# Hybrid attention block on one core: side work behind a step's transposes, an earlier split of the plain values, modulation sums closed later, more products ahead of the last heads

## The chip, the cores and the metric

The kernel runs on one core of one Trainium2 chip. The metric is device time in microseconds (us) of one execution; the time before is the median of three runs. The engines are called PE (matrix products and transposes, with PEld for its weight loads), DVE (vector), ACT (scalar), POOL (GpSimd) and SP (which issues the transfers).

## The reference

One layer of a backbone block over 512 latent tokens and 256 context tokens, width 1024, all in float32. What matters of it:

```
sh1, sc1, g1, sh2, sc2, g2 = split(silu(c) @ w_mod + b_mod, 6)
h, hc = modulate(rms_norm(x), sh1, sc1), modulate(rms_norm(ctx), csh1, csc1)
qa, ka, va, hy, qd, kd, vd = split(h @ w_in)          # and the context's from hc
ya = softmax(qa [ka_c, ka]^T) [va_c, va]              # 4 plain heads, 2 shared key/value heads
yd = (softmax(q1 k1^T) - lam softmax(q2 k2^T)) vd     # 4 differential heads, 768 keys
yh = hyena(hy)                                        # long convolutions
y  = concat(rms(ya), rms(yh), rms(yd) * 0.8) @ w_out
x  = x + g1 * y
a, v = split(modulate(rms_norm(x), sh2, sc2) @ w_up)
out = x + g2 * ((gelu(dwconv3(a)) * v) @ w_down)
```

Each differential head has two softmax components. "d" in the kernel's names stands for the differential heads, "a" for the plain ones, "h" for Hyena.

## The kernel before, in words

**Products.** Most products are made in three parts: each operand is split into a "hi" part in fp32r (a cast, mostly on ACT, `hi_of`, L72) and a "lo" part, what is left of it (a subtraction on DVE or POOL, `lo_of`, L80); `mm3` (L82 to L85) adds hi·hi, lo·hi and hi·lo. So whatever comes from PE as an operand of a later product takes the way PE, ACT (hi), DVE (lo), PE.

**Stages.** Filters and transforms of Hyena; then Hyena and the input projection woven together (chunks q0 to q7, each for the latent rows, L, and the context, C), to about 280 us; then the attention steps, to about 392; then the output projection with what is left of the heads; then the feed-forward half, from 439 us to the end.

**Modulation's sums.** The projections of c for g1, sh2 and sc2 are matrix-vector products. `mod2_step` (L715) makes one of 24 pieces each time it is called: it loads 512 KB of w_mod (mraw, two buffers), and DVE adds it, scaled, into macc (L732, eight to a column group). When a group is full, its closing products stand due: eight small PE matmuls (mc, L737), which add over the partitions, and an addition into mcol on DVE (L738). `MOD_AT` says how many pieces come per chunk. Before the change the closing comes two calls after the last piece, and the call between does nothing (`pause`).

**Early heads.** Three attention steps of the first differential head run inside the projection's chunks 6 and 7, with tiles named se (scores), mxe (maximum) and pe (exponential). Their scores have one PSUM buffer, so the scores of the next component wait until ACT has made the exponential of the last.

**Attention steps.** The steps are a list: 16 for the d heads (four heads, four blocks of 128 queries, two components each), then those of the a heads. The loop over n (L1141 to L1173) works in a pipeline: step n's scores and exponentials, the combination of the two components of step n-1 on POOL, the transposes of step n-3, the products with the values of step n-5. In the form for n < 16 a step is, for each component jj: scores on PE (sd, L745/L746), the maximum over 768 keys on DVE (mxd, L749), the exponential on ACT (pd, L750); and for each half of step n-3: three transposes on PE (Td, L1055) into one PSUM tile and ACT's copy of it into SBUF (atd, L72). `values` (L1072) is six matmuls into yd. From n = 16 on (`late`) the order is another one; the change doesn't touch it.

**Side work.** Beside the steps run generators, started at given steps, which `advance()` moves on by one `yield` each; it is called twice a step. They are: `prepare` (from `PREP_AT`: transposes of the next head's q and k, qTd, kT0d, kT1d, hi casts qhld and khd, lo's, transfers into the stacked tiles), `y_out` (transposes yT, hi and lo of a finished output Y), `finish_d` (ysbd, ynd, ysqd, s4d: the norm of a d head), `split_va` (from `VA_AT`: hi and lo of the plain heads' values, va into vas), and `finish_a`. Typically a generator's PE and ACT part falls into a step's first call and its DVE part into the second.

**PSUM.** All transposes, those of the steps (Td) and those of the side work (qT, kT, yT, yn), take tiles of one tag with three buffers (`ps_t`). Scores have two, the heads' outputs one.

**What sets the order.** Within the attention loop and the tail the instructions of PE, DVE and ACT run in the order in which the code issues them (`manual_schedule`); before it, in that of a scheduler with the code's order as its guide. POOL's and SP's rows are ordered by the framework. Each engine works through its row in order.

**Tail.** After the loop, 24 partial products of the output projection (`fill`, `accumulate`, three matmuls o each) are dealt out by `TAIL` between calls of `advance()`, so many ahead of each. In between, the last a head is finished: DVE multiplies yna by the row's norm sa (L1006), PE transposes it (yTa, L940), ACT and DVE make Y. Weights of the output projection are loaded and split in units (`wo_unit`: or, oh, ol); `WO_LO` names for each of eight units the engine of its lo, p for POOL and v for DVE.

Of the kernel before, what the change touches and what calls it, by code (L numbers as in the profile page):

```python
# [8 lines left out]
F32 = mybir.dt.float32  # L9
F32R = mybir.dt.float32r  # L10
AF = mybir.ActivationFunctionType
ALU = mybir.AluOpType
# [2 lines left out]
NOSYNC = mybir.DependencyInfo(mybir.DependencyClass.NoSync, mybir.DependencyReason.DATA)  # L15

P = 128
WO_LO = "ppppvvvv"

D_C, D_T, D_V = 1, 3, 5  # L20
LATE = 16
EARLY = 3
MOD_AT = (0, 0, 0, 2, 2, 2, 2, 2, 2, 2, 2, 2, 2, 2, 0, 0)
PREP_AT = (4, 7, 12, 17)
VA_AT = 13
HY_AT = (5, 6)
WO_AT = (24, 26, 28)
TAIL = (2, 0, 0, 0, 0, 0, 7, 0, 0, 2)
UP_AT, UP_AHEAD, UP_NEXT, UP_LAG = 4, 5, 5, 2
D = 1024  # L30
T = 512
# [13 lines left out]
def block_kernel(tc, x, ctxt, small, ffs, wmod1, wmod2, whyd, wqkvd, woutd, wupd, wdownd,  # L45
# [668 lines left out]

    def mod2_step():  # L715

        if m2s.pop("pause", False):
            return
        if "due" in m2s:
            m2s.pop("due")()  # L720
        n = m2s["n"]
        if n == m2s["end"]:
            return
        m2s["n"] = n + 1
        g, k = n // NK, n % NK
        r = m2s["pl"].tile([P, D], F32, tag="mr", bufs=2, name=f"mraw{g}{k}")
        dma(r, wmod2[g, k])
        if k == 0:
            m2s["a"] = m2s["pl"].tile([P, D], F32, tag="ma", bufs=1, name=f"macc{g}")
            V.tensor_scalar(m2s["a"], r, sv[:, 0:1], None, ALU.mult)  # L730
        else:
            V.scalar_tensor_tensor(m2s["a"], r, sv[:, k:k + 1], m2s["a"], ALU.mult, ALU.add)  # L732
        if k == NK - 1:
            def due(a=m2s["a"]):
                t0 = m2s["ps"](f"mc{g}")
                for i in range(NK):
                    T_.matmul(t0[:, 2 * i:2 * i + 2], a[:, i * P:(i + 1) * P], ones[:, 0:2], start=True, stop=True)  # L737
                V.tensor_tensor(mcol[:, g], t0[:, 0:16:2], cols[:, C_BM + 8 * g:C_BM + 8 * g + 8], ALU.add)  # L738
            m2s["due"], m2s["pause"] = due, True

    def scores(s, qs, ks, kz, j, tt):

# [240 lines left out]
    def finish_a(b, yps):  # L983
        V.reciprocal(rra[:, :, 2 * b:2 * b + 2], sta[:, :, 2 * b:2 * b + 2])
        ysb = y3(f"ysba{b}")
        S.copy(ysb, yps)
        yield
        yn0 = natural(f"a{b}", ysb)
        yield
        yn = att.tile([P, 4, 2, 64], F32, name=f"yna{b}")  # L990
        V.tensor_tensor(yn, yn0.rearrange("p (a j d) -> p a j d", a=4, j=2),
                        rra[:, :, 2 * b:2 * b + 2].unsqueeze(3).broadcast_to([P, 4, 2, 64]), ALU.mult)
        yield
        sq = y3(f"ysqa{b}").rearrange("p (a c) -> p a c", a=4)
        S.activation(sq, yn.rearrange("p a j d -> p a (j d)"), AF.Square)
        yield
        V.tensor_reduce(sa[:, b], sq, AX.X, ALU.add)
        yna[b] = yn
        if b == 1:
            V.tensor_tensor(sa[:, 0], sa[:, 0], sa[:, 1], ALU.add)  # L1000
            rstd_of(sa[:, 2], sa[:, 0], 256, 4)
            yield
            yield
            for b_ in range(2):
                yv = yna[b_].rearrange("p a j d -> p a (j d)")
                V.tensor_tensor(yv, yv, sa[:, 2].unsqueeze(2).broadcast_to([P, 4, P]), ALU.mult)  # L1006
                yield
                yield from y_out(b_, f"a{b_}", lambda tt: yv[:, tt])

# [89 lines left out]
    def wo_unit(n_):  # L1099
        r = wp.tile([P, D], F32, tag="wr", bufs=3, name=f"or{n_}")  # L1100
        dma(r, woutd[n_])
        if n_ in (2, 7):
            h = wx.tile([P, 2, D], F32R, tag="x", bufs=1, name=f"ox{n_}")
            h, l = h[:, 0], h[:, 1]
        else:
            pl, tg = (dp, "o") if n_ in (3, 4) else (wp, "w")
            h = pl.tile([P, D], F32R, tag=tg + "h", bufs=2, name=f"oh{n_}")
            l = pl.tile([P, D], F32R, tag=tg + "l", bufs=2, name=f"ol{n_}")
        hi_of(h, r, "a")
        lo_of(l, r, h, WO_LO[n_])  # L1110
        wo[n_] = h.rearrange("p (k c) -> p k c", k=2), l.rearrange("p (k c) -> p k c", k=2)

    def po_of(tt, n):
# [20 lines left out]
    while n < len(steps) + D_V:  # L1134
# [10 lines left out]
        if late:  # L1145
            if on(D_T):
                for hh in range(2):
                    transposes(n - D_T, held[n - D_T][0], hh)
                held.pop(n - D_T)
            if n - 1 in waiting:  # L1150
                held[n - 1] = waiting.pop(n - 1)()
            if on(D_C):
                combine(n - D_C, held[n - D_C])
            while later:
                later.pop(0)()
            advance()
            if on(D_V):
                values(n - D_V)
            if on(0):
                waiting[n] = front(n, 0)  # L1160
        else:
            held[n] = front(n, 0)()
            if on(D_C):
                combine(n - D_C, held[n - D_C])
            advance()
            if on(D_T):
                transposes(n - D_T, held[n - D_T][0], 0)
            held[n] += front(n, 1)()
            if on(D_T):
                transposes(n - D_T, held.pop(n - D_T)[0], 1)  # L1170
            if on(D_V):
                values(n - D_V)
        advance()  # L1173
# [302 lines left out]
```

## Time and profile before

| | |
|---|---|
| median of three runs (lowest, highest) | 819.24 us (816.74, 821.53) |
| the profiled execution's own time | 818.88 us |
| its span in the trace | 817.1 us |
| mean granted clock of PE | 0.981 |
| PE busy in the span | 95% |
| DVE, ACT, POOL busy | 58%, 39%, 25% |
| attention steps 3 to 15 (279.71 to 342.00) | 62.29 us, PE busy 51.87 |
| late attention steps (342.00 to 391.60) | 49.60 us, PE busy 49.24 |
| from there to 439.00 (tail, output projection) | 47.40 us, PE busy 45.10 |

A row of the timeline gives the start in us, the duration in us, the engine, the line, the operation, and what it writes and reads; xN means N alike in a row, whose duration is that of all. In square brackets stands how long the engine had been idle, and what ended that. A row of the waits reads: who waited, for what, us in total, how many times, the longest. A row of a stretch gives its bounds, its length, the busy us of each engine with the number of instructions, PE's granted clock (1.00 is full speed), the share of the transfers and GB/s; a row with one number ahead of the clock is for PE alone. Durations of rows that follow each other on one engine overlap by about 0.1 us, so costs are read from start to start. PE's ends are modelled.

### The profile page before, as it was taken

To read this page: it belongs to the slowest core of one execution; us is meant where nothing else is said; L and a number is where in the kernel's file an instruction comes from. 1 tells how busy PE (TensorE), PEld (TensorE's weight loads), DVE (VectorE), ACT (ScalarE), POOL (GpSimd) and SP (SyncE) were. 2 spreads that over 40 slices of the span, in tenths; PEclk is the share of its full clock that TensorE was granted. 3 is DMA by queue.
4 is the path that set the end of the run, shared out by engine and by line. 5 is a ranking of instruction groups with operands and counts; after the bars stand their busy time and mean duration, and the time that the engine had idled before them with its cause. 6 is when DMAs were issued, how large, how long until landed. Compare 5 with 4: busy or idle time off the path is not lost.

```text
span 817.1 us, 11113 instructions
## 1 busy us (share of the span) xinstructions
PE 776.7 (95%) x4334; PEld 655.9 (80%) x4334; DVE 476.5 (58%) x679; ACT 318.5 (39%) x546; POOL 201.7 (25%) x190
## 2 busy tenths in 40 slices
PE   5888999999998988899899999999999999999997
PEld 1246889999997877799788988888888888888886
DVE  5555578886876777778376594444444333333325
ACT  1464434323122477778254343332333232332320
POOL 0652506757950556622151000000000000000000
PEclk8698999999999999999999999999999999999999
DMA  8901232114675332412352183232223323232202
GB/s 326 384 3 59 96 129 79 53 31 152 219 231 188 85 90 66 116 26 79 129 187 75 52 270 104 91 103 103 91 89 103 103 77 104 78 104 99 82 26 103
DMA packets 30701, 93.68 MB, mean 115 GB/s; under 512 B 5639, under 2 KB 8022, under 8 KB 29625
## 3 DMA queue, kind: packets, MB, share of 16 engines
q1 hardware_dynamic: 30649, 92.98, 34.4%
q8 instruction: 34, 0.56, 0.3%
q14 instruction: 18, 0.15, 0.1%
HBM read 83.79 MB, written 2.10 MB: 105 GB/s over the span
## 4 chain that ended last, share of the span: by engine, by line
PE 81%; DVE 8%; ACT 4%; POOL 2%; DMA 2%; issue 2%; SPq 0%; ACTq 0%; DVEq 0%; POOLq 0%
PE u L84 5%; PE u L83 5%; PE u L85 5%; PE dn L85 5%; PE dn L84 5%; PE dn L83 5%; PE uv L83 2%; PE ua L85 2%; PE uv L84 2%; PE uv L85 2%; PE ua L83 2%; PE ua L84 2%; PE yd L1072 2%; DMA mraw<-in_dram 2%; PE f L384 2%
## 5 line engine op out<-in xcount | busy, mean ns | idle before, releaser
L80 DVE TENSOR_TENSOR ul<-ur,uh 128x1024 fp32r<-128x1024 f32 x62 | 75.9, 1224 | 101.9 <-ACT uh L72 101.0
L72 ACT CAST uh<-ur 128x1024 fp32r<-128x1024 f32 x66 | 69.2, 1051 | 116.3 <-PE u L84 90.6
L83 PE MATMUL u<-h2h,uh 128*128 128x512 f32 (+1 forms) x224 | 81.2, 363 | 0.0
L85 PE MATMUL u<-h2h,ul 128*128 128x512 f32 (+1 forms) x224 | 80.3, 359 | 0.0
L84 PE MATMUL u<-h2l,uh 128*128 128x512 f32 (+1 forms) x224 | 80.3, 359 | 0.0
L84 PE MATMUL dn<-ul,gh 128*128 128x512 f32 x176 | 69.6, 396 | 0.0
L85 PE MATMUL dn<-uh,gl 128*128 128x512 f32 x176 | 69.6, 396 | 0.0
L83 PE MATMUL dn<-uh,gh 128*128 128x512 f32 x176 | 69.3, 396 | 0.0
L80 DVE TENSOR_TENSOR gl<-gT,gh 128x512 fp32r<-128x512 f32 x22 | 15.2, 690 | 60.1 <-ACT gh L72 60.1
L84 PEld LDWEIGHTS u<-h2l,uh 128*128 128x128 f32 x224 | 42.3, 189 | 6.2
L83 PEld LDWEIGHTS u<-h2h,uh 128*128 128x128 f32 x224 | 42.2, 189 | 6.2
L85 PEld LDWEIGHTS u<-h2h,ul 128*128 128x128 f32 x224 | 42.3, 189 | 6.2
L732 DVE SCALAR_TENSOR_TENSOR macc<-mraw,sv,macc 128x1024 f32<-128x1024 f32 x28 | 37.5, 1341 | 8.0 <-DMA mraw<-in_dram 7.8
L80 DVE TENSOR_TENSOR wl<-wr,wh 128x1024 fp32r<-128x1024 f32 x22 | 30.3, 1380 | 19.4 <-ACT wh L72 19.3
L72 ACT CAST gh<-gT 128x512 fp32r<-128x512 f32 x22 | 13.5, 620 | 70.1 <-PE dn L84 70.1
L85 PEld LDWEIGHTS dn<-uh,gl 128*128 128x128 f32 x176 | 33.2, 188 | 8.1
L83 PEld LDWEIGHTS dn<-uh,gh 128*128 128x128 f32 x176 | 33.1, 188 | 8.1
L84 PEld LDWEIGHTS dn<-ul,gh 128*128 128x128 f32 x176 | 33.1, 188 | 8.1
L72 ACT CAST wh<-wr 128x1024 fp32r<-128x1024 f32 x22 | 22.9, 1046 | 39.6 <-issue 11.1
L83 PE MATMUL uv<-h2h,uh 128*128 128x512 f32 x80 | 31.2, 390 | 0.2 <-ACT uh L72 0.2
L83 PE MATMUL ua<-h2h,uh 128*128 128x512 f32 x80 | 31.3, 392 | 0.0
L84 PE MATMUL uv<-h2l,uh 128*128 128x512 f32 x80 | 31.2, 390 | 0.0
(741 smaller groups left out, 2183.1 us busy)
## 6 DMA issues: line engine op xcount, KB each, us to landing
ur<-in_dram SPq DMA_DIRECT2D x66, 512.0 KB, 3.2
mraw<-in_dram SPq DMA_DIRECT2D x32, 512.0 KB, 4.5
wr<-in_dram SPq DMA_DIRECT2D x22, 512.0 KB, 3.4
mraw<-in_dram SPq DMA_DIRECT2D x8, 1024.0 KB, 7.6
or<-in_dram SPq DMA_DIRECT2D x8, 512.0 KB, 4.8
xo<-in_dram SPq DMA_DIRECT2D x6, 512.0 KB, 8.9
x<-in_dram SPq DMA_DIRECT2D x4, 512.0 KB, 5.5
out_dram<-x SPq DMA_DIRECT2D x8, 256.0 KB, 2.0
```

Of the source, the lines that this page charges most:

```text
L72: return S.copy(dst, src)
L80: return e.tensor_tensor(dst, src, f(hi), ALU.subtract)
L83: i0 = T_.matmul(o, ah, bh, start=start, stop=False)
L84: T_.matmul(o, ah, bl, start=False, stop=False)
L85: return i0, T_.matmul(o, al, bh, start=False, stop=stop)
L384: T_.matmul(t0, h2[:, a * P:(a + 1) * P], fw3s[:, d], start=True, stop=True)
L732: V.scalar_tensor_tensor(m2s["a"], r, sv[:, k:k + 1], m2s["a"], ALU.mult, ALU.add)
L1072: T_.matmul(o, Vt[2 + h][:, kt], at[:, kt], start=kt == 0, stop=kt == 5)
```

## The change

Five edits; in the order of the program:

- **Modulation.** The pause goes; a full group's closing waits eight calls (two for the last group), while the next group's pieces go on. For that, two sums are alive at once, and the second one's macc lies in another tile (tag x).
- **Plain values.** `split_va` starts at step 10, not 13.
- **Side work.** In the steps below 16 the first `advance()` moves from between the two components' work to behind the second transposes.
- **Tail.** Ten partial products, not seven, stand ahead of the first transposes of yna, and four, not two, ahead of the second.
- **Output weights.** The lo of unit 3 goes from POOL to DVE; the lo's of units 4 to 7 are issued behind the last multiplication of yna.

```diff
-WO_LO = "ppppvvvv"
+WO_LO = "pppvvvvv"
...
-VA_AT = 13
+VA_AT = 10
...
-TAIL = (2, 0, 0, 0, 0, 0, 7, 0, 0, 2)
+TAIL = (2, 0, 0, 0, 0, 0, 10, 0, 0, 4)
...
-        if m2s.pop("pause", False):
-            return
         if "due" in m2s:
-            m2s.pop("due")()
+            m2s["wait"] -= 1
+            if not m2s["wait"]:
+                m2s.pop("due")()
...
-            m2s["a"] = m2s["pl"].tile([P, D], F32, tag="ma", bufs=1, name=f"macc{g}")
+            if g == 1:
+                m2s["a"] = wx.tile([P, 2, D], F32, tag="x", bufs=1, name=f"macc{g}")[:, 0]
+            else:
+                m2s["a"] = m2s["pl"].tile([P, D], F32, tag="ma", bufs=1, name=f"macc{g}")
...
-            m2s["due"], m2s["pause"] = due, True
+            m2s["due"], m2s["wait"] = due, 8 if g < 3 else 2
...
-                V.tensor_tensor(yv, yv, sa[:, 2].unsqueeze(2).broadcast_to([P, 4, P]), ALU.mult)
+                state["yna"] = V.tensor_tensor(yv, yv, sa[:, 2].unsqueeze(2).broadcast_to([P, 4, P]), ALU.mult)
...
-        lo_of(l, r, h, WO_LO[n_])
+        if n_ < 4:
+            lo_of(l, r, h, WO_LO[n_])
+        else:
+
+            with tc.issue_after(state["yna"].ins):
+                lo_of(l, r, h, WO_LO[n_])
...
             if on(D_C):
                 combine(n - D_C, held[n - D_C])
-            advance()
             if on(D_T):
                 transposes(n - D_T, held[n - D_T][0], 0)
             held[n] += front(n, 1)()
             if on(D_T):
                 transposes(n - D_T, held.pop(n - D_T)[0], 1)
+            advance()
             if on(D_V):
                 values(n - D_V)
```

PE's row in step 6, before: sd12None are the scores of step 6 (its two components follow each other), kT1d and yTh side work, Td03None the transposes of step 3, yd the values of step 1.

```order
L745 MATMUL sd12None_3080<-ksX,X_2750 128x512
L746 MATMUL sd12None_3080<-X_2751,X_2750 128x512
L745 MATMUL sd12None_3080<-ksX,X_2750 128x256
L746 MATMUL sd12None_3080<-X_2751,X_2750 128x256
L669 MATMUL kT1d_3094<-ident,kd_1290 128x128 x3
L940 MATMUL yTh_3099<-ident,yhn 128x128 x4
L1055 MATMUL Td03None_3107<-ident,pd03None_2949 128x128 x3
L745 MATMUL sd12None_3112<-ksX,X_2750 128x512
...
L1055 MATMUL Td03None_3121<-ident,pd03None_2949 128x128 x3
L1072 MATMUL yd_3072<-atd00None_2952,vd_2629 128x256 x3
```

The same place now:

```order
L749 MATMUL sd12None_3080<-X_2757,X_2756 128x256
L1058 MATMUL Td03None_3094<-ident,pd03None_2949 128x128 x3
L748 MATMUL sd12None_3099<-ksX,X_2756 128x512
...
L1058 MATMUL Td03None_3108<-ident,pd03None_2949 128x128 x3
L669 MATMUL kT1d_3113<-ident,kd_1290 128x128 x3
L943 MATMUL yTh_3118<-ident,yhn 128x128 x4
L1075 MATMUL yd_3072<-atd00None_2952,vd_2625 128x256 x3
```

The two side transposes have gone from ahead of both Td03None to behind both.

ACT's row from the first exponential of step 6 to that of step 7, before: pd12None are the exponentials, khd and Y the side work's hi casts, atd02None the copies of Td03None.

```order
L750 ACTIVATE pd12None_3086,std_2972<-sd12None_3080,mxd12None_3085 128x768
L72 CAST khd_3038<-kT1d_3094 128x384
L947 ACTIVATE Y_3104<-yTh_3099,cols 128x256 x2
L72 COPY atd02None_3052<-Td03None_3107 128x3x128
L750 ACTIVATE pd12None_3118,std_2972<-sd12None_3112,mxd12None_3117 128x768
L72 COPY atd02None_3052<-Td03None_3121 128x3x128
L750 ACTIVATE pd13None_3143,std_2972<-sd13None_3137,mxd13None_3142 128x768
```

And now:

```order
L753 ACTIVATE pd12None_3086,std_2972<-sd12None_3080,mxd12None_3085 128x768
L72 COPY atd02None_3038<-Td03None_3094 128x3x128
L753 ACTIVATE pd12None_3105,std_2972<-sd12None_3099,mxd12None_3104 128x768
L72 COPY atd02None_3038<-Td03None_3108 128x3x128
L72 CAST khd_3058<-kT1d_3113 128x384
L950 ACTIVATE Y_3123<-yTh_3118,cols 128x256 x2
L753 ACTIVATE pd13None_3143,std_2972<-sd13None_3137,mxd13None_3142 128x768
```

The casts have gone from ahead of the first copy to behind the second; on DVE the rows of these steps stand as before, the lo's of khd and Y (kzY and Y) between the second maximum of a step and the first of the next.

DVE's row around the early heads, before: macc are modulation's sums, mxe the maxima of the early heads' components, mcol the end of group 1's closing.

```order
L74 COPY vd_2630<-q6L_2412 128x256
L738 TENSOR_TENSOR mcol<-mc_2452,cols 128x8
L730 TENSOR_SCALAR macc_2464<-mraw_2462,sv 128x1024
L732 SCALAR_TENSOR_TENSOR macc_2464<-mraw_2466,sv,macc_2464 128x1024
L74 COPY vd_2630<-q6C 128x256
L80 TENSOR_TENSOR wl_2643<-wr_2473,wh_2642 128x1024
L732 SCALAR_TENSOR_TENSOR macc_2464<-mraw_2547,sv,macc_2464 128x1024
L749 TENSOR_REDUCE mxe_2664<-se_2658 128x1
L732 SCALAR_TENSOR_TENSOR macc_2464<-mraw_2550,sv,macc_2464 128x1024
L732 SCALAR_TENSOR_TENSOR macc_2464<-mraw_2667,sv,macc_2464 128x1024
L749 TENSOR_REDUCE mxe_2700<-se_2694 128x1
```

And now:

```order
L74 COPY vd_2626<-q6C 128x256
L80 TENSOR_TENSOR wl_2639<-wr_2469,wh_2638 128x1024
L752 TENSOR_REDUCE mxe_2660<-se_2654 128x1
L735 SCALAR_TENSOR_TENSOR macc_2285<-mraw_2462,sv,macc_2285 128x1024
L735 SCALAR_TENSOR_TENSOR macc_2285<-mraw_2543,sv,macc_2285 128x1024
L735 SCALAR_TENSOR_TENSOR macc_2285<-mraw_2546,sv,macc_2285 128x1024
L735 SCALAR_TENSOR_TENSOR macc_2285<-mraw_2663,sv,macc_2285 128x1024
L752 TENSOR_REDUCE mxe_2696<-se_2690 128x1
L741 TENSOR_TENSOR mcol<-mc_2711,cols 128x8
```

Four sums stand between the first and the second maximum, where two stood, and group 1's closing has gone behind the second.

## The prediction

> **What bounds the kernel now.** First the page, for the engine that carries the span; then the busy time by stage, to see where that engine is not full; then the waits, for what it waits on there; last the timeline of one step. The page says that PE is busy nearly throughout:
>
> ```profile
> PE 776.7 (95%) x4334; PEld 655.9 (80%) x4334; DVE 476.5 (58%) x679; ACT 318.5 (39%) x546; POOL 201.7 (25%) x190
> ```
>
> By stage (first the stretch in us and its length, then busy us of PE, PEld, DVE, ACT, POOL, and PE's granted clock):
>
> ```profile
> 279.71:342.00 62.29, 51.87 (x316) 44.73 (x316) 46.82 (x88) 46.16 (x103) 41.31 (x33) 1.00 0.35 87
> 342.00:391.60 49.60, 49.24 (x367) 45.92 (x366) 37.36 (x66) 38.15 (x82) 11.46 (x9) 1.00 0.15 47
> ...
> 439.00:817.10 378.10, 373.41 (x1748) 310.15 (x1746) 171.76 (x213) 115.54 (x151) 1.17 (x3) 1.00 0.30 99
> ```
>
> The feed-forward half, which the change does not touch, is PE at work. The attention steps 3 to 15 are where PE has 10.4 us idle (62.29 - 51.87), with DVE and ACT some 75% busy. The waits name what ended PE's idle time (total us, times, longest):
>
> ```profile
> PE Td03None L1055 <- ACT atd02None L72: 1.8, 1, 1.8
> ...
> PE mc L737 <- DVE macc L732: 1.9, 1, 1.9
> ...
> PE Td21None L1055 <- ACT atd20None L72: 1.7, 1, 1.7
> ...
> PE Td22None L1055 <- ACT ynd L960: 1.2, 1, 1.2
> ...
> PE Td02None L1055 <- ACT atd02None L72: 1.1, 1, 1.1
> ```
>
> A second transpose waits until ACT has copied the first one out. Step 6 shows why (all engines, start and duration):
>
> ```profile
> 293.03 0.96 DVE L749 TENSOR_REDUCE mxd12None<-sd12None 128x1 f32<-128x768 f32 x1 [0.80 <-PE sd12None L746]
> ...
> 293.60 0.49 PE L1055 MATMUL Td03None<-ident,pd03None 128*128 128x128 f32 x3
> ...
> 294.02 0.90 ACT L750 ACTIVATE pd12None<-sd12None,mxd12None 128x768 f32<-128x768 f32 x1 [2.33 <-DVE mxd12None L749]
> ...
> 294.92 0.47 ACT L72 CAST khd<-kT1d 128x384 fp32r<-128x384 f32 x1
> 295.27 0.85 ACT L947 ACTIVATE Y<-yTh,cols 128x256 fp32r<-128x256 f32 x2
> ...
> 295.70 1.11 DVE L80 TENSOR_TENSOR kzY<-kT1d,khd 64x384 fp32r<-64x384 f32 x2
> 296.00 0.49 ACT L72 COPY atd02None<-Td03None 128x384 f32<-128x384 f32 x1
> ...
> 296.55 0.55 PE L1055 MATMUL Td03None<-ident,pd03None 128*128 128x128 f32 x3 [1.75 <-ACT atd02None L72]
> ...
> 296.85 0.88 DVE L950 SCALAR_TENSOR_TENSOR Y<-yTh,cols,Y 128x256 fp32r<-128x256 f32 x2
> ...
> 299.13 0.96 DVE L749 TENSOR_REDUCE mxd13None<-sd13None 128x1 f32<-128x768 f32 x1 [1.40 <-PE sd13None L746]
> ```
>
> Side transposes (kT1d, yTh) hold two of three transpose slots in PSUM. Td03's first half is done by 294.1, but ACT casts the side work first and copies it only at 296.00, so PE stands 1.75 us. The maximum of the next step then waits for PE (1.40 us): the loop closes over PE, ACT and PE again.
>
> **The change part by part.** *Side work behind the transposes.* On ACT the hi casts now stand behind both exponentials and both copies. DVE's row stays as it was: both maxima, the side work's lo's, then the next step's first maximum (mx0). The lo's need the hi's, so a step becomes one chain: mx0, exp, copy, exp, copy, hi, lo, next mx0. How long it is up to the hi is seen in step 10, which has no side cast on ACT; the other two rows are the mx0 of steps 4 and 15:
>
> ```profile
> 283.78 0.96 DVE L749 TENSOR_REDUCE mxd10None<-sd10None 128x1 f32<-128x768 f32 x1 [1.09 <-PE sd10None L746]
> ...
> 312.23 0.96 DVE L749 TENSOR_REDUCE mxd22None<-sd22None 128x1 f32<-128x768 f32 x1
> ...
> 336.68 0.96 DVE L749 TENSOR_REDUCE mxd33None<-sd33None 128x1 f32<-128x768 f32 x1
> ```
>
> ```profile
> 315.42 0.49 ACT L72 COPY atd12None<-Td13None 128x384 f32<-128x384 f32 x1
> ```
>
> The second copy starts 3.19 us after mx0, and the next ACT instruction can start about 0.36 later (295.27 - 294.92 for a cast of that size): 3.55 us. What hangs behind it:
>
> ```profile
> 301.07 0.57 ACT L72 CAST qhld<-qTd 128x512 fp32r<-128x512 f32 x1
> ...
> 328.50 0.81 ACT L72 CAST vas<-va 128x768 fp32r<-128x768 f32 x1
> ```
>
> ```profile
> 301.68 0.69 DVE L80 TENSOR_TENSOR qhld<-qTd,qhld 128x512 fp32r<-128x512 f32 x1
> ...
> 311.25 0.69 DVE L965 TENSOR_REDUCE s4d<-ysqd 128x4 f32<-128x512 f32 x1
> ...
> 329.71 0.95 DVE L80 TENSOR_TENSOR vas<-va,vas 128x768 fp32r<-128x768 f32 x1
> ```
>
> - Steps 4 and 7 (one q): 301.68 + 0.69 - 301.07 = 1.30, less 0.05 overlap: 4.8 us each.
> - Step 8 (one k): cast 0.47, handover, two lo's 1.15 (296.85 - 295.70): 5.2.
> - Steps 5 and 6 (k and two Y): k's lo's until 1.65, Y's lo's 0.88: 3.55 + 2.5 = 6.05 each.
> - Steps 9, 13, 14 (k, and the d heads' norm): lo's until 1.65, the small sums 0.98 (312.23 - 311.25): 6.2 each.
> - Steps 10 and 11, to which the split of the plain values moves: 0.81 + 0.05 + 0.95: 5.36 each. Here it loses its old place in two steps that were long anyway.
> - Step 12 (Y and q): two casts of 0.57, lo 0.69, handovers: 5.5.
>
> Sum 9.6 + 5.2 + 12.1 + 18.6 + 10.7 + 5.5 = 61.7 us from mx0 of step 4 to that of step 15. Before it is 336.68 - 283.78 = 52.9. So the waits in the rows above go, but the chain is late next: **+8.8 us**. PE's work a step has no say in it. The late form that follows is full on PE (49.24 of 49.60 us), so nothing is caught up there. Bounds: handovers 0.3 us a step shorter give +5.5, 0.2 longer +11.
>
> [...]
>
> *Modulation's sums.* The products mc of column group 1 now stand between later projection products, and PE's 1.9 us wait for macc goes. But four sums (macc) now stand on DVE between the maxima of early heads 0 and 1, and DVE waits for their loads. The clock of these:
>
> ```profile
> 246.54 1.28 DVE L732 SCALAR_TENSOR_TENSOR macc<-mraw,sv,macc 128x1024 f32<-128x1024 f32 x1 [0.59 <-DMA mraw<-in_dram]
> ...
> 256.21 1.28 DVE L732 SCALAR_TENSOR_TENSOR macc<-mraw,sv,macc 128x1024 f32<-128x1024 f32 x1
> ...
> 260.75 1.28 DVE L732 SCALAR_TENSOR_TENSOR macc<-mraw,sv,macc 128x1024 f32<-128x1024 f32 x1 [1.21 <-DMA mraw<-in_dram]
> 261.95 0.95 DVE L749 TENSOR_REDUCE mxe<-se 128x1 f32<-128x768 f32 x1
> ```
>
> ```profile
> 264.04 0.50 PE L745 MATMUL se<-ks0d,qsd 128*128 128x512 f32 x1 [0.81 <-ACT pe L750]
> ```
>
> ```profile
> 264.04:279.71 15.67, 15.67 (x127) 1.00 0.49 134
> ```
>
> With two load buffers a sum starts 3.26 us after the one before the last ended (260.75 - 257.49) and takes 1.28. Seven sums of group 2 now come ahead of the second mxe. The last of group 1 ends at 247.82; two loads are in flight, so every second sum ends 4.54 us (3.26 + 1.28) after the one before the last: the second at 252.36, the fourth at 256.9, the sixth at 261.44, and the seventh 1.28 later, at 262.7. That is the earliest; with the copies and a lo that stand between I take 263.3. So mxe starts there and not at 261.95, the scores se of the next head follow 2.1 later as now, and from these PE is full until the steps begin (last row): **+1.4 us** (+0.3 to +3, and -1.9 if mxe isn't late). PE has then waited over 3 us ahead of se, which bears on the clock:
>
> ```profile
> 249.50:252.90 3.40, 3.40 (x17) 0.50 0.53 169
> ```
>
> Now half a clock for 3.4 us follows the wait for macc; it costs 1.7 us, and is likely to come behind se instead, where PE is the bound. Since it may also fall into the wait, I take **+0.6** (0 to 1.7).
>
> *The tail.* Three more products stand ahead of the first transposes of yna and two more ahead of the second:
>
> ```profile
> 397.61 0.39 PE L83 MATMUL o<-oh,Y 128*128 128x512 f32 x1
> ...
> 398.07 0.40 PE L85 MATMUL o<-oh,Y 128*128 128x512 f32 x1
> 399.91 0.63 PE L940 MATMUL yTa<-ident,yna 128*128 128x128 f32 x4 [1.44 <-DVE yna L1006]
> ...
> 402.80 0.63 PE L940 MATMUL yTa<-ident,yna 128*128 128x128 f32 x4 [0.86 <-DVE yna L1006]
> ```
>
> A product takes 0.7 us (three matmuls 0.23 apart), so three cover 2.1 of the 1.44 and two cover 1.4 of the 0.86: **-2.3 us**. The lo of output weight 3 goes from POOL to DVE ahead of yna, while that of weight 4 goes behind it. This costs nothing while those products cover DVE; without that cover up to 1.3 of the 2.3 would be given back. The load that now waits for a later lo has products of the whole projection ahead of its use: nothing.
>
> Sum: 8.8 + 1.4 + 0.6 - 2.3 = +8.5. The profiled execution took 818.88 us (its span is 817.1, to the end of the last stretch above); 827.4 for it, and since the median of the three runs is 0.36 above it, **827.7 us**.
>
> **Rivals.** *A, faster.* The slots are the bound and the chain has slack: ACT and DVE take the lo's beside PE's work, and mx0 isn't held. Then the four waits of the rows go, 5.8 us, macc's 1.9 and the tail's 2.3: 818.88 - 10.0 + 0.36 = 809.2. It decides if the lo's end ahead of the next step's scores, that is if hi and lo together take no more than what PE's own work in a step leaves behind the 3.55, some 0.8 us where it is 4.35 (step 6, the row below); the shortest pair takes 1.3. For it speaks that the waits are there. [...] Chance 0.12.
>
> *B, slower still.* In the chain PE has some 4.35 us of work (row below) in a step of 6.05, so 1.7 idle, and in the shorter steps 1 to 2; if the clock falls behind them as it did behind macc's 1.87 us, each fall costs up to 1.7. Against it: step 6 of before kept its clock with a wait of 1.75:
>
> ```profile
> 291.94:298.04 6.10, 4.35 (x29) 3.81 (x28) 4.40 (x9) 3.73 (x9) 2.72 (x2) 1.00 0.26 54
> ```
>
> Two to four falls give 831 to 834.5. Chance 0.15. [...]
>
> *C, no change.* The chain is shorter by the lower bound (+5.5), mxe isn't late (-1.9) and the tail gives 2.3: +1.3, 820.5. Chance 0.13.
>
> **How the numbers follow.** The forecast has 0.60, B 0.15, C 0.13, A 0.12. A measurement of this kernel can tell about 0.5% from no change, 4.1 us. Slower by over that: forecast and B, 0.75; within: C, 0.13; faster: A, 0.12. The range runs from 820 (5.5 - 1.9 - 2.3 above the time before, C's own value) to 834 (B's, or 11 for the chain with 3 and 1.7 for the sums, less 2.3, which is 832.6); it leaves out A and the far ends.
>
> **What would show it.** Right: mx0 of steps 4 to 15 spread over about 61.7 us, with side lo's right ahead of them on DVE and side hi's behind the second copy on ACT; no Td that waits for atd in the second half of a step; mxe01 at about 263 and PE's se behind it; no wait of yTa for yna. Wrong: mx0 that still waits for PE's scores (A), or a spread near 53 us; clock stretches of 0.50 in the steps (B).

## The result, and the profile after

The changed kernel took 831.52 us (median of four runs, 830.72 to 834.83) where the kernel before took 819.25 (816.74 to 821.53, four runs): a ratio of 1.0155 with a 95% interval of 1.0129 to 1.0181, or +12.7 us by the ratio (12.3 between the medians). The profiled execution took 832.28 us with a span of 830.5. PE is busy for the same share of a longer span (first part of the page):

```profile
PE 785.4 (95%) x4334; PEld 663.1 (80%) x4334; DVE 477.2 (57%) x680; ACT 317.8 (38%) x546; POOL 198.8 (24%) x189
```

To see where the time went, a few marks are taken that both programs pass. Of the changed kernel, first on DVE the first maxima of steps 4 and 15, then on PE the first scores of the late steps (sa), the first product of the output projection (o) and the first of the up-projection (u):

```profile
287.50 0.96 DVE L752 TENSOR_REDUCE mxd10None<-sd10None 128x1 f32<-128x768 f32 x1 [1.09 <-PE sd10None L749]
...
351.11 0.96 DVE L752 TENSOR_REDUCE mxd33None<-sd33None 128x1 f32<-128x768 f32 x1
```

```profile
357.95 0.69 PE L748 MATMUL sa<-ksY,qsY 128*128 128x512 f32 x1
...
407.63 0.40 PE L83 MATMUL o<-oh,Y 128*128 128x512 f32 x1
...
455.60 0.37 PE L83 MATMUL u<-h2h,uh 128*128 128x256 f32 x1
```

The same three on PE in the kernel before:

```profile
342.01 0.58 PE L745 MATMUL sa<-ksY,qsY 128*128 128x512 f32 x1
...
391.57 0.40 PE L83 MATMUL o<-oh,Y 128*128 128x512 f32 x1
...
442.21 0.36 PE L83 MATMUL u<-h2h,uh 128*128 128x256 f32 x1
```

| stretch (us) | before | after | difference | forecast |
|---|---|---|---|---|
| to the first mc | 222.18 | 221.75 | -0.4 | 0 |
| first mc to mx0 of step 4 | 61.60 | 65.75 | +4.2 | +2.0 |
| mx0 of step 4 to mx0 of step 15 | 52.90 | 63.61 | +10.7 | +8.8 |
| mx0 of step 15 to first sa | 5.33 | 6.84 | +1.5 | 0 |
| first sa to first o | 49.56 | 49.68 | +0.1 | 0 |
| first o to first u | 50.64 | 47.97 | -2.7 | -2.3 |
| first u to the end of the span | 374.9 | 374.9 | 0.0 | 0 |

The differences add up to the 13.4 us between the two spans.

Step 6 of the changed kernel, against the rows of before (all engines; start, duration):

```profile
298.31 0.95 DVE L752 TENSOR_REDUCE mxd12None<-sd12None 128x1 f32<-128x768 f32 x1
...
299.30 0.90 ACT L753 ACTIVATE pd12None<-sd12None,mxd12None 128x768 f32<-128x768 f32 x1 [2.22 <-DVE mxd12None L752]
...
300.19 0.47 ACT L72 COPY atd02None<-Td03None 128x384 f32<-128x384 f32 x1
300.55 0.91 ACT L753 ACTIVATE pd12None<-sd12None,mxd12None 128x768 f32<-128x768 f32 x1
300.71 0.66 PE L943 MATMUL yTh<-ident,yhn 128*128 128x128 f32 x4 [1.63 <-ACT atd02None L72]
...
301.44 0.48 ACT L72 COPY atd02None<-Td03None 128x384 f32<-128x384 f32 x1
301.80 0.50 ACT L72 CAST khd<-kT1d 128x384 fp32r<-128x384 f32 x1
302.17 0.87 ACT L950 ACTIVATE Y<-yTh,cols 128x256 fp32r<-128x256 f32 x2
...
302.33 1.12 DVE L80 TENSOR_TENSOR kzY<-kT1d,khd 64x384 fp32r<-64x384 f32 x2 [1.88 <-ACT khd L72]
...
303.49 0.88 DVE L953 SCALAR_TENSOR_TENSOR Y<-yTh,cols,Y 128x256 fp32r<-128x256 f32 x2
...
304.28 0.94 DVE L752 TENSOR_REDUCE mxd13None<-sd13None 128x1 f32<-128x768 f32 x1
```

This is the forecast chain. The second copy starts 3.13 us after mx0 and the cast khd 3.49 after it. The next mx0 has no idle time ahead of it and no releaser: it comes straight behind Y's lo, though its scores were ready at 303.4. No Td of steps 4 to 15 waits for atd any more. But the wait for a slot is still there: it has moved from Td03 (1.75 us) to the side tile yTh (1.63), and PE catches it up ahead of DVE.

What PE waits for in the changed kernel, and what it waited for in the kernel before, are different things (who waits, for what, us in total, times, longest):

```profile
PE se L748 <- ACT pe L753: 3.7, 1, 3.7
...
PE yTh L943 <- ACT atd02None L72: 3.4, 2, 1.8
...
PE qTa L638 <- ACT atd20None L72: 2.7, 1, 2.7
...
PE Td31None L1058 <- ACT atd30None L72: 2.3, 1, 2.3
...
PE ynd L932 <- ACT atd12None L72: 1.8, 1, 1.8
```

Neither mc nor yTa is among them any more. The first row is the early heads. DVE's row there (maxima mxe, sums macc):

```profile
254.50 0.95 DVE L752 TENSOR_REDUCE mxe<-se 128x1 f32<-128x768 f32 x1
255.37 2.59 DVE L735 SCALAR_TENSOR_TENSOR macc<-mraw,sv,macc 128x1024 f32<-128x1024 f32 x2
259.94 1.28 DVE L735 SCALAR_TENSOR_TENSOR macc<-mraw,sv,macc 128x1024 f32<-128x1024 f32 x1 [1.98 <-DMA mraw<-in_dram]
262.44 1.28 DVE L735 SCALAR_TENSOR_TENSOR macc<-mraw,sv,macc 128x1024 f32<-128x1024 f32 x1 [1.21 <-DMA mraw<-in_dram]
263.64 0.95 DVE L752 TENSOR_REDUCE mxe<-se 128x1 f32<-128x768 f32 x1
```

The second mxe starts at 263.64, where 263.3 was forecast. PE waits ahead of the second scores, and the products of group 1's closing now come behind these (in the kernel before they ran from 247.97 to 250.15, ahead of them):

```profile
256.52 0.80 PE L748 MATMUL se<-ks1d,qsd 128*128 128x512 f32 x1 [3.75 <-ACT pe L753]
...
260.53 3.41 PE L740 MATMUL mc<-ones,macc 128*128 128x2 f32 x16
```

And the clock (stretch, length, PE's busy us, granted clock):

```profile
255.70:269.40 13.70, 12.88 (x56) 0.50 0.35 118
317.20:320.60 3.40, 3.40 (x11) 0.50 0.30 66
334.40:337.80 3.40, 3.32 (x11) 0.52 0.00 0
354.80:358.30 3.50, 3.46 (x11) 0.52 0.64 249
```

One stretch of half clock lies behind the early heads' wait of 3.75 us, four times as long as the 3.40 us of before, and three more behind the waits of steps 9, 12 and 16 for slots (1.83, 2.69 and 2.35 us). The fall of before stood behind PE's wait for macc:

```profile
247.97 2.18 PE L737 MATMUL mc<-ones,macc 128*128 128x2 f32 x16 [1.87 <-DVE macc L732]
```

### The profile page after: what moved, and what is told of

Its sections match the earlier page's. It is cut to its first block, busy times and chain, and to the rows that moved or that the text cites. A ratio compares the mean times of both kernels' runs of the same rounds, so it can differ in the third digit from the quotient of the medians.

```text
span 830.5 us, 11117 instructions
## 1 busy us (share of the span) xinstructions
PE 785.4 (95%) x4334; PEld 663.1 (80%) x4334; DVE 477.2 (57%) x680; ACT 317.8 (38%) x546; POOL 198.8 (24%) x189
## 4 chain that ended last, share of the span: by engine, by line
PE 56%; ACT 4%; DVE 3%; issue 1%; ACTq 0%
PE u L84 5%; PE u L83 5%; PE u L85 5%; PE dn L84 5%; PE dn L85 5%; PE dn L83 5%; PE uv L83 2%; PE ua L85 2%; PE uv L84 2%; PE uv L85 2%; PE ua L83 2%; PE ua L84 2%; PE o L85 2%; PE o L84 2%; PE o L83 2%; PE yd L1075 2%
```

## The experiments

Each ratio below is to the kernel before, run beside the experiment; a difference in us is that ratio's share of 819.

Step lengths in us, from the first maximum of a step to that of the next, in one profiled execution each; the last column is from mx0 of step 15 to the first sa (step 16 in the text; "late, paused" is the late closing with the pause):

```
step               4    5    6    7    8    9   10   11   12   13   14 |  sum   | to sa
before           3.16 6.09 6.10 3.78 3.68 5.64 3.25 3.44 6.11 5.66 5.99| 52.90  | 5.33
forecast         4.8  6.05 6.05 4.8  5.2  6.2  5.36 5.36 5.5  6.2  6.2 | 61.7   |
after            4.80 6.01 5.97 4.79 5.23 6.82 5.60 5.30 6.71 6.23 6.15| 63.61  | 6.84
side moved alone 4.80 6.74 5.98 4.79 5.24 6.30 3.10 3.59 5.57 7.10 7.03| 60.24  | 6.85
side back        3.16 6.15 6.10 3.78 3.68 5.64 5.59 5.00 8.30 5.54 5.13| 58.07  | 5.33
split alone      3.16 6.09 6.11 3.78 3.68 5.64 5.58 4.99 8.30 5.54 5.12| 57.99  | 5.33
modulation back  4.81 6.76 5.98 4.80 5.24 6.30 5.60 5.30 6.36 6.36 6.17| 63.68  | 5.33
lo behind max    3.10 5.57 6.36 7.58 5.05 8.02 4.75 5.59 6.56 6.53 5.05| 64.16  | 7.80
filled steps     4.81 6.01 5.97 4.80 5.23 6.30 5.59 5.30 6.72 6.23 6.17| 63.13  | 6.30
late, paused     4.80 6.78 5.98 4.80 5.23 6.30 5.59 5.31 5.56 6.22 6.17| 62.74 | 6.74
side between     3.55 4.98 4.99 3.78 3.98 5.04 3.36 3.36 5.05 5.84 5.99| 49.92  | 5.33
```

**The side work moved, alone.** The kernel before with the first `advance()` behind the second transposes.

```diff
-            advance()
             if on(D_T):
                 transposes(n - D_T, held[n - D_T][0], 0)
...
                 transposes(n - D_T, held.pop(n - D_T)[0], 1)
+            advance()
```

> The kernel before with one edit alone: the side work moved behind the second transposes. Chain theory: the maxima mx0 of steps 4 to 15 spread over the length that exp, copy, exp, copy, hi and lo have in a row, about 62 us before any clock loss where they took 52.9 before; with the split of the plain values still in steps 13 and 14 these two get longer and steps 10 and 11 shorter. With up to three half-clock stretches as in the changed kernel, 10 to 13 us slower than the kernel before: 829 to 832. Rival (the loss comes from the early split or the modulation sums together with the move): under 5 us slower, 820 to 824.

828.86 us, ratio 1.0099 (1.0068 to 1.0131), +8.1 us. The steps spread over 60.24 us. So the move by itself costs as much as two thirds of the net loss. Where the split stands in steps 13 and 14 they take 7.1 and 7.0 us, and without it in the changed kernel 6.2; steps 10 and 11, with nothing to cast, keep 3.10 and 3.59. That is the chain counted by what hangs on it. The time lies just under the range that was expected.

**The side work back.** The changed kernel with the same lines the other way round.

```diff
+            advance()
             if on(D_T):
                 transposes(n - D_T, held[n - D_T][0], 0)
...
                 transposes(n - D_T, held.pop(n - D_T)[0], 1)
-            advance()
```

> The changed kernel with the side work back in its old place, all other edits kept. Chain theory: the spread of mx0 falls from 63.6 to about 53 us and the late steps lose no clock, so 11 to 13 us less than the changed kernel, 819 to 821; what is left against the kernel before is modulation's +3.7 and the tail's -2.7. Rival (the order of the side work matters little, the early split is what costs): over 825.

826.91 us, ratio 1.0090 (1.0066 to 1.0115). This is about 5 us less than the changed kernel, not 11 to 13, and the rival's prediction (over 825) holds: the early split costs by itself. What the move costs so depends on what stands beside it: 8.1 us alone, 5.3 beside the other edits.

**Modulation back.** The changed kernel with the old `mod2_step`.

```diff
+        if m2s.pop("pause", False):
+            return
         if "due" in m2s:
-            m2s["wait"] -= 1
-            if not m2s["wait"]:
-                m2s.pop("due")()
+            m2s.pop("due")()
...
-            m2s["due"], m2s["wait"] = due, 8 if g < 3 else 2
+            m2s["due"], m2s["pause"] = due, True
```

> The changed kernel with the old closing of modulation's sums (pause, closing two calls later). Theory (four sums between the maxima of the first two early components delay the second score set, and the clock falls behind PE's wait): 3.7 us less than the changed kernel, about 828, and no half clock of 13 us after the early heads begin. Rival (the later closing itself is a gain and the delay comes from elsewhere in the projection): no less than the changed kernel, 831 to 833.

828.52 us, ratio 1.0102 (1.0076 to 1.0129): 4.3 us less than the changed kernel by the ratios, where 3.7 was expected. From the first mc to mx0 of step 4 it takes 60.80 us where the changed kernel takes 65.75, and its stretch of half clock there is 3.5 us long, as before.

**The tail alone.** The kernel before with `TAIL`, `WO_LO` and the later lo's behind yna.

```diff
-WO_LO = "ppppvvvv"
+WO_LO = "pppvvvvv"
...
-TAIL = (2, 0, 0, 0, 0, 0, 7, 0, 0, 2)
+TAIL = (2, 0, 0, 0, 0, 0, 10, 0, 0, 4)
...
+            with tc.issue_after(state["yna"].ins):
+                lo_of(l, r, h, WO_LO[n_])
```

> The kernel before with the tail's edits alone: ten and four products ahead of the last transposes, weight 3's lo on DVE, the later lo's behind yna. Theory: the two waits of PE go and nothing takes their place, 2.3 to 2.7 us less than before, 816.5 to 817. Rival (the products only move, and their weights' later lo's bring a wait behind them): within 1 us of before.

816.16 us over ten runs, ratio 0.9966 (0.9947 to 0.9984), -2.8 us. This edit does what it was expected to do, and makes a kernel a little faster than both.

**The lo behind the next maximum.** The changed kernel with the closing `advance()` of a step moved.

```diff
             held[n] += front(n, 1)()
+            advance(prev)
...
-        advance()
+        prev = list(running)
+        if n >= LATE - 1:
+            advance()
```

(`advance(prev)` moves only generators that were running when the step before ended.)

> The changed kernel with one thing else: the second move of the side work (its lo's on DVE above all) no longer closes a step but stands behind the second maximum of the next step, so that no maximum waits for a lo that waits for a cast. Chain theory: the spread of mx0 over steps 4 to 15 falls from 63.6 us to what PE, ACT and DVE need by themselves, 48 to 55, and with it the clock stretches; 8 to 14 us less than the changed kernel, 818 to 824. Rival (the slots in PSUM, now held longer by the side work, are the bound): the spread stays at 60 or more, 828 to 836.

833.41 us, ratio 1.0166 (1.0136 to 1.0196): nothing gained, spread 64.16 us. The expectation from the chain failed and the rival held. PE's rows of this kernel in step 7, second transposes:

```profile
304.36 0.55 PE L1058 MATMUL Td10None<-ident,pd10None 128*128 128x128 f32 x3 [1.47 <-ACT atd10None L72]
...
305.13 0.71 PE L638 MATMUL qTd<-ident,qd 128*128 128x128 f32 x4 [0.22 <-DVE kzY L80]
```

The maxima no longer wait for a lo, but a side tile that waits longer for its lo holds its slot into the next step. So the second transposes wait for ACT's first copy as in the kernel before, and now qTd waits for kz's lo as well. A second bound stands behind the first. Its size is not shown cleanly: three falls of the clock lie in steps 7, 9 and 12 of this run (3.5 us at half clock each). At the 0.5 to 1.5 us that a fall costs below, the spread would be some 60 to 63 us without them (an estimate), where the changed kernel without its falls has 61.9.

**The split alone.** The kernel before with one number changed.

```diff
-VA_AT = 13
+VA_AT = 10
```

> The kernel before with the split of the plain values at step 10 and nothing else. Theory (steps 10 and 11 were bound by PE at 3.3 us, and a cast and a lo between their maxima make them as long as the chain; steps 13 and 14 were long for other reasons and win less): spread of mx0 57 to 59 us for 52.9, 4 to 6 us slower than before. Rival (the two places are worth the same): within 1.5 us of before.

825.36 us, ratio 1.0080 (1.0059 to 1.0101), +6.6 us, a little more than the 4 to 6 that were expected; the spread of 57.99 lies within what was expected. Steps 10 to 12 take 5.6, 5.0 and 8.3 us, steps 13 and 14 win 1.0 together. Steps 10 and 11 are as long as in the changed kernel, but not by its chain. In the old order the lo of vas runs beside POOL's combination (first DVE, then POOL, of this kernel):

```profile
317.93 2.58 DVE L80 TENSOR_TENSOR vas<-va,vas 128x768 fp32r<-128x768 f32 x1
```

```profile
317.36 2.33 POOL L756 TENSOR_TENSOR pd21None<-pd21None,pd21None 128x768 f32<-128x768 f32 x1
```

It takes 2.58 us instead of 0.95, and ends 0.82 after POOL does (320.51 against 319.69). In the changed kernel the same lo, behind the chain, takes 1.24 and 0.96; the one of 1.24 again ends 0.82 after a sum on POOL (326.80 against 325.98). What steps 10 and 11 would take without POOL beside the lo was not run. Step 12, 2.2 us longer than before, has a wait of 2.76 us and then runs 5.6 us at half clock:

```profile
327.50:334.50 7.00, 5.56 (x18) 0.51 0.34 76
```

Together with the moved side work the split costs less (spread 60.24 to 63.61) than alone (52.90 to 57.99).

**Filled steps.** The changed kernel with products in PE's waits of steps 9, 12 and 16.

```diff
+        for _ in range(FILL.get((n, hh), 0)):
+            T_.matmul(t0[:, 384:512], ident, ident, start=True, stop=True)
         tv = t0[:, :384].rearrange("p (i q) -> p i q", i=3)
```

> The changed kernel with 54 products of 128 columns of the identity with itself, written to unused columns of transposes' tiles where PE stands idle: 14 behind the second transposes in step 9, 20 in step 12, 20 between the two transposes of step 16. Clock theory (the half clock that follows these waits lengthens steps 9, 12 and 16 by 0.6, 1.2 and 1.5 us): the three stretches of 0.50 are gone, the spread of mx0 falls to 61.5 to 62.5 us, and the time by 2 to 3.5, 828 to 829.5. Rival (these steps are long by their waits for slots, and the half clock falls into the waits): no change within 1 us.

832.40 us, ratio 1.0166 (1.0143 to 1.0189): no change. The three stretches are gone, as expected, and step 9 takes 6.30 us for 6.82. But a product of this kind shows as two records (40 for 20 in step 12), so there was twice the filling that was meant, and steps 12 (6.72) and 16 (6.30) stay long by the filling itself. As a test of the price it is inconclusive. A better one came by chance: the clock does not fall behind the same wait each time. The run with modulation back has the waits of the changed kernel in steps 9 and 16, and one of 1.71 us in step 5 (1.76 there):

```profile
290.17 0.89 PE L940 MATMUL yTh<-ident,yhn 128*128 128x128 f32 x4 [1.71 <-ACT atd02None L72]
...
313.02 0.66 PE L929 MATMUL ynd<-ident,ysbd 128*128 128x128 f32 x4 [1.84 <-ACT atd12None L72]
...
349.11 0.55 PE L1055 MATMUL Td31None<-ident,pd31None 128*128 128x128 f32 x3 [2.34 <-ACT atd30None L72]
```

```profile
290.50:294.00 3.50, 3.50 (x11) 0.52 0.09 20
```

It lost the clock in step 5 (6.76 us for 6.01) and again in step 12, and kept it in 9 (6.30 for 6.82) and 16 (5.33 for 6.84), where the six products yd behind the waits took 1.46 us each time, against 2.77 at half clock in step 5. For step 12 the late closing with the pause (below) gives the price, since it has the same steps and the same wait there and kept its clock. First the changed kernel, then that one:

```profile
334.48 1.12 PE L638 MATMUL qTa<-ident,qa 128*128 128x128 f32 x4 [2.69 <-ACT atd20None L72]
...
338.73 0.96 DVE L752 TENSOR_REDUCE mxd31None<-sd31None 128x1 f32<-128x768 f32 x1 [1.07 <-PE sd31None L749]
```

```profile
333.65 0.66 PE L638 MATMUL qTa<-ident,qa 128*128 128x128 f32 x4 [2.69 <-ACT atd20None L72]
...
336.75 0.95 DVE L756 TENSOR_REDUCE mxd31None<-sd31None 128x1 f32<-128x768 f32 x1
```

```profile
331.20:336.80 5.60, 3.15 (x19) 1.00 0.00 0
```

At full clock the maximum that ends step 12 comes straight behind the lo's and the step takes 5.56 us, as forecast; at half clock it waits 1.07 us for PE's scores and the step takes 6.71. A fall in the steps so costs 0.5 to 1.5 us, and in the changed kernel's profiled execution those of steps 9, 12 and 16 make 0.5, 1.2 and 1.5, together 3.2. Without them its eleven steps would spread over 61.9 us.

**Filled early heads.** The changed kernel with products ahead of the second early scores, in the scores' own tile.

```diff
+        if e == 1:
+            for _ in range(32):
+                T_.matmul(state["se"][:, 768:896], ident, ident, start=True, stop=True)
-        s = pp(f"se{n}{jj}")
+        s = state["se"] = pp(f"se{n}{jj}")
```

> The changed kernel with 32 products of 128 columns of the identity with itself, written to unused columns of the scores' tile ahead of the second early component's scores, where PE waits 3.75 us. Clock theory (the half clock of 13.7 us that follows this wait costs some 2 us of the 3.7): no half clock there, the first maxima of the steps 1.5 to 2.5 us earlier, 829 to 830. Rival (the delay is the maximum's wait for four sums alone, and the half clock falls into it): no change within 1 us.

836.75 us, ratio 1.0223 (1.0196 to 1.0250), some 5 us slower than the changed kernel. The filling waited for ACT like the scores, and came behind the wait:

```profile
259.60 7.41 PE L771 MATMUL se<-ident 128*128 128x128 f32 x64 [2.92 <-ACT pe L753]
```

The clock stayed whole by the length of its 64 records (0.116 us each; the 28 transposes of the next run, at a granted clock of 1.00, took 0.115 each), but PE was 7.4 us late instead. It says nothing on the price of the clock.

**Filled early heads, another tile.** 28 transposes into a tile of their own at the same place.

```diff
+        if e == 1:
+            t0 = pt("fill")
+            for _ in range(28):
+                T_.transpose(t0[:, :128], ident, ident)
```

> The changed kernel with 28 transposes of the identity into a tile of its own, ahead of the second early component's scores, where PE waits about 3.7 us; they wait for nothing (in the run before this one the products waited for ACT like the scores, and came behind the wait). Clock theory: no half clock of 13 us behind the early heads' first wait, steps 1.5 to 2.5 us earlier against the first closing's place, 829 to 830.5. Rival (the half clock falls into the second maximum's wait for the sums): no change within 1 us.

833.97 us, ratio 1.0177 (1.0147 to 1.0208): no gain where 1.5 to 2.5 us were expected. The ratio is 1.8 us above the changed kernel's, and the intervals overlap, so the rival (no change) stands. The filling ran in the wait, and the long stretch was gone:

```profile
255.38 3.22 PE L772 MATMUL fill<-ident 128*128 128x128 f32 x28
...
267.55 0.50 PE L748 MATMUL se<-ks0d,qsd 128*128 128x512 f32 x1 [3.12 <-ACT pe L753]
```

At full clock (1.00 from the filling to 264.5) PE reaches the third scores early and waits 3.12 us for the second maximum, which the sums hold until 265.46. Step 4 begins 65.31 us after the first mc, for 65.75. So most of the long half clock lay in a wait anyway, though the test is not clean: the clock fell to 0.50 for 3.4 us behind that new wait, and for 3.4 us once more ahead of step 4.

**The late closing, with the pause.** The changed kernel with the skipped call put back for the first three groups.

```diff
+        if m2s.pop("pause", False):
+            return
         if "due" in m2s:
...
+            if g < 3:
+                m2s["pause"] = True
```

> The changed kernel with the pause put back, the late closing kept: two of modulation's sums, not four, between the maxima of the first two early components. Theory (the sums ahead of the maximum make the delay, not the closing's place): the second early maximum comes 4 to 5 us after the first and not 9, the steps' start is 3 to 5 us earlier, 827 to 829. Rival (the late closing does it, by the clock or by its products between later projection products): no less than 831.

829.77 us, ratio 1.0115 (1.0082 to 1.0147): 3.3 us less than the changed kernel by the ratios, whose intervals overlap, and between the two expectations. The second maximum comes 3.72 us after the first (9.14 in the changed kernel), and step 4 begins 63.79 us after the first mc (65.75; before 61.60). That second difference alone shows little, since four traces with the changed closing, without pause or filling there, spread from 63.83 to 66.19 us there. From the second scores to step 4, where the sums stand, the traces do part: 24.4 to 24.5 us in six with the old closing, 29.9 to 31.0 in those four, 28.1 and 28.3 in two with the pause (this run and the last one below). So the sums between the maxima explain 1.5 to 2.9 us of the 5.4 to 6.6 that are lost there. The rest stays with the late closing: PE still waits 3.8 us ahead of the second scores, and 6.8 us of half clock begin within that wait (granted clock 0.50 from 256.8 to 263.6).

**The side work between, with the tail.** The tail's edits, and the first `advance()` between the first transposes and the second scores.

```diff
-            advance()
             if on(D_T):
                 transposes(n - D_T, held[n - D_T][0], 0)
+            advance()
             held[n] += front(n, 1)()
```

> The kernel before with the tail's edits and the side work moved half as far: behind the first transposes and ahead of the second component's scores. ACT then makes the first copy ahead of the casts, which frees its slot early, and the casts still stand ahead of the second exponential, so that a lo is ready before the next step's scores. Theory (the order of ACT's row decides, by the slot on one side and the lo on the other): the spread of mx0 falls below the 52.9 us of before, to 47 to 51, and the time to 811 to 815, less than the 816 of the tail's edits alone. Rival (any move of the side work away from the head of the step costs): spread over 53 us, 817 or more.

815.70 us over ten runs, ratio 0.9951 (0.9929 to 0.9973), -4.0 us. The spread falls to 49.92 us, 3.0 less than before. Step 6 of this kernel:

```profile
294.22 0.47 ACT L72 COPY atd02None<-Td03None 128x384 f32<-128x384 f32 x1
294.58 0.49 ACT L72 CAST khd<-kT1d 128x384 fp32r<-128x384 f32 x1
294.75 0.55 PE L1055 MATMUL Td03None<-ident,pd03None 128*128 128x128 f32 x3 [0.65 <-ACT atd02None L72]
...
295.11 1.12 DVE L80 TENSOR_TENSOR kzY<-kT1d,khd 64x384 fp32r<-64x384 f32 x2
```

The copy comes ahead of the cast, so the slot is free 1.1 us sooner than before; the cast comes ahead of the second exponential, so the lo runs while ACT is at that. By the steps this is better than the tail alone, as expected; by the times 815.7 and 816.2 can't be told apart (the intervals overlap for the most part), and the time came out above the 811 to 815 that was expected.

**The same, with the late closing and the pause.** The kernel of the last experiment with the `mod2_step` of the one before it.

```diff
+            m2s["wait"] -= 1
+            if not m2s["wait"]:
+                m2s.pop("due")()
...
+            m2s["due"], m2s["wait"] = due, 8 if g < 3 else 2
+            if g < 3:
+                m2s["pause"] = True
```

> The kernel with the side work between first transposes and second scores and with the tail's edits, and beside these the late closing with the pause kept. Theory (the wait of PE for macc of 1.9 us goes, and no sum is added ahead of a maximum; the half clock behind that wait goes too): 1.5 to 3.5 us less than the same kernel with the old closing. Rival (PE only reaches the next score set earlier and waits there): no difference within 1 us.

816.13 us over twelve runs, ratio 0.9956 (0.9938 to 0.9974): no difference from the kernel without it. PE's wait for macc is gone, and PE waits 3.7 us ahead of the second scores instead. The rival holds.

## Why the prediction was right, point by point

**Direction and range** were right: +8.5 us was forecast, 827.7 us in a range of 820 to 834, and 831.52 was measured. It lies where rival B put the time. By the trace, what the sum of 8.5 lacks of 13.4 is 2.2 in modulation, 1.9 in the steps, 1.5 behind step 15, and -0.7 in the rest; 3.2 of it are falls of the clock in the steps, which the sum left to B.

**The side work behind the transposes.** The chain was right in its mechanism, and step by step to 0.1 us in eight of the eleven (table above). The sum came out as 63.6 for 61.7. Steps 9 and 12 are long by 0.6 and 1.2, and that is the clock: with the same waits and a whole clock they take 6.30 and 5.56, and the chain then has ten of eleven steps to 0.1 us and 61.9 for its sum. So "PE's work a step has no say in it" holds only at full clock: at half, the maxima that end steps 9 and 12 waited 0.55 and 1.07 us for PE's scores. The move alone and the side work between show that the order on ACT and DVE decides; the lo behind the maximum shows that the slots stand behind it. Rival A's condition, that the chain have slack, was wrong, but its slots are as real as the chain (1.63 us for yTh in step 6).

**The early split** was priced at 2 us for each of steps 10 and 11 and at a small gain in 13 and 14. Within the changed kernel that holds (5.6 and 5.3 us). That the split costs as much in the old order too, where no chain holds it but its lo runs against POOL, was not seen.

**Modulation** is the term that was mis-sized: +2.0 forecast (1.4 and 0.6 for the clock), +4.2 measured between the two traces, 4.3 by putting the old closing back. (The kernel before has the longest of six traces with the old closing, 60.47 to 61.60 us, their mean is 61.0; of the four with the changed closing three lie some 5 above that, one 3.) "Mxe starts there and not at 261.95" was right (263.64). Wrong was where PE waits: not over 3 us ahead of the third scores, but 3.75 ahead of the second. There the clock fell 0.8 us ahead of the scores' own start, and it stayed at half for 13.7 us, while PE caught up what it had lost. With the sums back in twos, 1.5 to 2.9 us come back behind the second scores. The length of the half clock is not what decides: the side work back has the same sums and only two falls of 3.4 and 3.5 us there, and takes 65.73 us from the first mc to step 4, as the changed kernel does (65.75); the filling in another tile, with two falls of 3.4 us, takes 65.31. How much of the rest is the clock at all and how much the new place of the closing stays open: the two fillings could not part them, since without the half clock PE waited at the next scores.

**The clock in the steps** was rival B, with a chance of 0.15 and two to four falls of up to 1.7 us. The profiled execution has three, and they cost 3.2 us together: B came true beside the forecast. "Step 6 kept its clock with a wait of 1.75" was true and no evidence: another run lost it behind 1.71 us and kept it behind 2.34. So B should have had the larger chance, given the six waits of 1.6 to 2.7 us that stand in the steps of the new order.

**The tail** was right: -2.3 forecast, -2.7 in the trace, -2.8 alone.

Rival C, no change, was not near.

## What to carry to other kernels

Moving the casts behind the exponential freed one engine's row here and tied the next (in step 6 PE's wait of 1.75 us ahead of Td03 went, and DVE waited 1.88 us for khd): in a loop that runs over two engines in fixed order, write out what stands between one step's first instruction and the next one's on each, and sum it; here that gave ten of eleven steps to 0.1 us wherever the clock held. Ask of each wait that goes what holds the same thing next (the slot behind the lo, the next scores behind the closing): three edits that took a wait away brought another (1.63 us for 1.75 at the slots of step 6, 3.75 for 1.87 at the closing, and 1.47 for a slot where the maxima no longer waited for a lo). A copy that frees a shared buffer goes first, a cast whose lo is wanted goes second, and both ahead of the long exponential (0.47, 0.49 and 0.93 us in step 6): that order gave the shortest steps of the three (49.9 us, against 52.9 with the casts first and 60.2 with them last), though the time can't be told from that of the tail's edits alone.

## What the runs showed of the hardware

With modulation back the granted clock fell behind PE's wait of 1.71 us in step 5 (0.52 over 3.50 us) and stayed whole behind 2.34 us in the same run (the six products yd behind that wait took 1.46 us; at half clock 2.77). A wait of 1.83 us lost it in the changed kernel (0.50 over 3.40 us), one of 1.84 did not with modulation back (yd 1.46). The same wait of 2.69 us lost it in the changed kernel (0.52 over 3.40 us) and not in the late closing with the pause (1.00 over 5.60 us). A fall lasted 3.4 to 3.5 us in most places, but 6.3 us with the side work moved alone (0.50 from 347.5 to 353.8), about 6.9 in step 12 of the split alone (0.51 over 7.00 us), 6.8 around the second early scores in the two runs with the pause, 13.7 behind those scores in the changed kernel, with PE busy for 12.88 of it, and some 10 there in two other runs (the lo behind the maximum, the filled steps); what holds it there is not settled.

A subtraction on DVE with both operands in SBUF (vas, 128x768) took 2.58 us beside POOL's sum of two tiles of that size and 0.95 without it, and ended 0.82 us behind POOL's end. Why it takes longer there no run shows.
